# Windowed attention in an encoder block: query preparation and value split placed behind the score products in each step's source order

## The chip, the cores and the metric

The kernel runs on one core of a Trainium2 chip. The metric is the device time of one execution in microseconds (us), as the median of several runs. A core has a TensorE (PE) for matrix products, a VectorE (DVE), a ScalarE (ACT), a GpSimd (POOL) and a queue (SP) from which most DMA transfers are issued. Matrix products write to PSUM, and ACT or DVE must copy the results out before a PSUM tile can be used again.

## What is computed

One block of a bidirectional encoder: 1024 tokens, width 1024, all in float32. The block has a gated linear attention (branch A), a windowed softmax attention (branch B), and a gated feed-forward part. The change lies in branch B:

```python
q = _rope(_rms_norm(q.reshape(bsz, s, SWA_HEADS, hd), q_g), pos)      # 8 heads of 128
k = _rope(_rms_norm(k.reshape(bsz, s, hkv, hd), k_g), pos)            # 2 heads of 128
kc, vc = context(k), context(v)          # blocks of 128 keys: the block before, its own, the next
scores = jnp.einsum("bnqhgd,bnkhd->bnhgqk", qb, kc) * (hd ** -0.5)
scores = jnp.where(mask, scores, -jnp.inf)               # +-128 window
m = jnp.maximum(scores.max(axis=-1, keepdims=True), sink)
p = jnp.exp(scores - m)
denom = p.sum(axis=-1, keepdims=True) + jnp.exp(sink - m)
o = jnp.einsum("bnhgqk,bnkhd->bnqhgd", p / denom, vc)
```

## The kernel before

**Precision.** The products run in a fast float32 form. Each operand is split into a high part (written by ACT) and a low part (the difference, written by DVE), and three products are summed: high by high, high by low, low by high.

**The order of the whole.** The block's input projections come first (partly by a seven-product scheme), then the gated linear attention, then the windowed attention, then the output projections of both branches, then the feed-forward part. Projections that the attention stages need late (queries, keys and values of branch B, a gate of branch A) are kept as generators in a list `dense`; the attention stages draw dense matmuls from it, so that PE has work while a step of the attention waits for other engines.

**The windowed attention (lines 828 to 1040).** It works on 16 units n: two key-value heads g, and eight blocks t of 128 queries, four query heads together. A software pipeline of 22 steps runs them. In step t stand:

- `k_load`, `a_load` (lines 880 and 887): DMA loads of keys, values and queries, for the next steps.
- `k_prep` (892), the split of values: `vSh` on ACT (L894) and `vSl` on DVE (L895), for steps 0 to 7. The parts are read by `a_out` four steps later at the earliest.
- `a_prep` (905), the preparation of the queries of unit t-1: square on ACT (L866), sum over the row on DVE (L867), the inverse root `rs` in two small ACT and four small DVE instructions (L98 to L104), then four DVE operations that apply the norm's gain and the rotation (L912, L914, L916, L917), which write `qn`. The inverse root is not applied to the query; it enters later as the scale of the exponential.
- `a_turn` (919), unit t-2: four transposes of `qn` on PE (L923) into a PSUM tile, then the split `sqh` (ACT, L926) and `sql` (DVE, L927). `k_turn` (897) does the same with the keys of block t-1 (L900, L902, L903).
- `a_scores` (931), unit t-3, four stages, one for each head: three products on PE (L76, the line of the helper `mm`) into a PSUM tile; then one DVE instruction (L941) adds the window's mask, writes the scores `p` to SBUF and takes the row maximum `mx`. The stage of the last head also holds the softmax: small DVE operations on the maxima (L948 to L952), one small and four large exponentials on ACT (L953, L956), the sum `dn` (L958) and its reciprocal `rd` (L960) on DVE, and four multiplications on POOL (L962).
- `a_probs` (964), unit t-5, three stages, one for each key block: four transposes of `p` on PE (L973), then `ph` (ACT, L976) and `pl` (DVE, L977).
- `a_out` (980), unit t-5: six or nine products of probabilities and values (L76), a copy `sob` on ACT (L987), and four DMA stores.

The PSUM tiles of scores, turned queries, turned keys, turned probabilities and outputs come from one pool of four tiles (`ch`); the dense matmuls have four others (`mm`). The scores, the raw queries, the values and `qn` have two buffers each.

**What sets the order.** A list `order` ranks the stages of one step, and `slot` runs them in that rank and puts a share of the step's dense matmuls (15 in steps 2 to 18) behind each stage:

```python
for j, f in enumerate(stages):
    f()
    t = n * (j + 1) // len(stages)
    fill(t - done)
    done = t
```

On PE the instructions stand in just this order (`manual_schedule`). On DVE, ACT, POOL and SP the compiler's planner orders them: it walks through time by its own estimates and gives each engine, whenever it is free, the first instruction in source order whose inputs and buffers are ready. So on these engines the source order is a preference and the result can differ from it; on the chip each engine then runs its list strictly in order. A step has 10 stages in steps 3 and 4, 14 in steps 5 to 7, 12 in step 8, 11 in steps 9 to 15 and 10 in step 16.

Of the kernel before, what the change touches and what calls it, by code (L numbers as in the profile page):

```python
# [30 lines left out]
def body(tc, i, out):  # L31
    nc = tc.nc
    with ExitStack() as root:
# [846 lines left out]
        def k_load(t):  # L880
            raws[t] = sw.tile([P, 256], F32, tag="kvr", name=nm("kvr"))
            need(("skv", t))
            nc.sync.dma_start(out=raws[t], in_=scr["skv", t][:, 256:512])
            keys[t] = sw.tile([P, 2, P], F32, tag="key", name=nm("key"))
            nc.sync.dma_start(out=keys[t].rearrange("p a b -> p (a b)"), in_=scr["key", t])
# [127 lines left out]
        for n in range(2 * KT):  # L1013
# [9 lines left out]
                if n:  # L1023
                    todo[n - 1].append((k_load, n))
            todo[n].append((a_load, g, t))
        order = (a_probs, k_prep, a_prep, a_scores, a_turn, k_turn, a_out, k_load, a_load)
        k_load(0)
        with tc.manual_schedule(engines={mybir.EngineType.PE}):
            for t, v in enumerate(todo):
# [507 lines left out]
```

## Time and profile before

| what | value |
|---|---|
| median of 3 runs | 1645.83 us (1645.22 to 1646.64) |
| profiled execution, its own time | 1645.61 us |
| its span, first to last instruction | 1643.8 us |
| granted TensorE clock, mean | 1.000 |
| DMA, mean over the span | 160 GB/s |
| windowed attention, about | 565 to 740 us |

In the profile a row such as `L76 PE MATMUL ch<-kTh,sqh` names the line, the engine, the operation and the tiles by the program's names without their numbers. The number in square brackets is the idle time of the engine just before the instruction, with the instruction that ended it. In the attention stage step 4 begins on PE at about 581 us, step 5 at 590.7, step 6 at 600.6, step 7 at 611.8, step 8 at 622.7, step 10 at 642.8, step 14 at 678.2 and step 16 at 698.9 (each from step 5 on begins with the transposes L973). Rows of PE overlap, since matmuls are pipelined, so the time that a matmul takes is read from the starts of neighbours.

### The profile page before, as it was taken

Reading aid. Unit: us, or ns where it says so; the run is one execution under the profiler, and the core shown is the slowest. Engines: PE = TensorE matmul, PEld = TensorE weight load, DVE = VectorE, ACT = ScalarE, POOL = GpSimd, SP = SyncE. Lnnn points to the kernel's source line nnn. Section 1 sums busy time; section 2 is a strip of 40 time slices with the busy share of each in tenths; the row PEclk is TensorE's granted clock in tenths of the full one; section 3 lists DMA queues with packets and bytes.
Section 4 is the critical chain, followed back from the end, with each engine's and each line's share of the span. In section 5 each row is a group of like instructions: output and inputs, shape, how many; then the busy total and the mean of one; then the engine's idle time right before and its main releaser. Section 6 shows DMA issues by size and latency. Waiting matters only on the chain.

```text
span 1643.8 us, 23281 instructions
## 1 busy us (share of the span) xinstructions
PE 1626.0 (99%) x7588; PEld 1346.0 (82%) x7588; DVE 1251.4 (76%) x2559; ACT 842.6 (51%) x1762; POOL 76.0 (5%) x68
## 2 busy tenths in 40 slices
PE   9999999999999989999999999999999999999999
PEld 7888888888888778888888888888888888888887
DVE  8866665589986598867885678887777778779655
ACT  8622224468998666665554557333333333354442
POOL 0000000000000034540000000000000000000000
PEclk9999999999999999999999999999999999999999
DMA  7554334475554633248765544443334443596433
GB/s 238 176 178 148 115 122 135 173 250 173 179 161 129 191 108 97 77 138 280 225 205 175 168 146 145 140 149 109 109 115 147 142 147 129 177 341 193 149 98 119
DMA packets 168010, 262.91 MB, mean 160 GB/s; under 512 B 19324, under 2 KB 52860, under 8 KB 167888
## 3 DMA queue, kind: packets, MB, share of 16 engines
q1 hardware_dynamic: 167888, 261.42, 49.8%
q8 instruction: 60, 0.98, 0.2%
q14 instruction: 62, 0.51, 0.1%
HBM read 187.93 MB, written 73.42 MB: 159 GB/s over the span
## 4 chain that ended last, share of the span: by engine, by line
PE 84%; DVE 9%; ACT 4%; DMA 2%; issue 1%; POOL 1%; SPq 0%; ACTq 0%; DVEq 0%
PE mm L76 23%; PE mm L306 9%; PE mm L308 9%; PE mm L307 9%; PE mm L1350 7%; PE ch L1350 5%; PE ch L76 4%; PE ch L306 4%; PE ch L308 4%; PE ch L307 4%; PE ch L460 3%; PE mm L460 2%; ACT p L956 1%; DVE wl L72 1%; DVE cs L655 1%
## 5 line engine op out<-in xcount | busy, mean ns | idle before, releaser
L298 ACT ACTIVATE wh<-ws 128x512 fp32r<-128x512 f32 x132 | 83.3, 632 | 195.9 <-PE mm L307 102.2
L70 ACT ACTIVATE wh<-wr 128x512 fp32r<-128x512 f32 x202 | 124.9, 626 | 87.4 <-PE mm L76 54.9
L72 DVE TENSOR_TENSOR wl<-wr,wh 128x512 fp32r<-128x512 f32 x202 | 137.7, 686 | 26.8 <-ACT wh L70 26.4
L299 DVE TENSOR_TENSOR wl<-ws,wh 128x512 fp32r<-128x512 f32 x132 | 90.5, 686 | 22.7 <-ACT wh L298 22.6
L298 ACT ACTIVATE wh<-wr 128x512 fp32r<-128x512 f32 x69 | 43.6, 632 | 124.8 <-issue 49.7
L962 POOL TENSOR_SCALAR p<-p,rd 128x384 f32<-128x384 f32 (+1 forms) x64 | 75.8, 1202 | 657.1 <-DMA qr<-sq 587.2
L298 ACT ACTIVATE wh<-a 128x512 fp32r<-128x512 f32 x64 | 40.5, 633 | 91.4 <-PE ch L1350 42.3
L76 PE MATMUL mm<-wh,xl 128*128 128x512 f32 x192 | 83.1, 433 | 0.0
L76 PE MATMUL mm<-wh,xh 128*128 128x512 f32 x192 | 79.6, 415 | 0.0
L76 PE MATMUL mm<-wl,xh 128*128 128x512 f32 x192 | 79.6, 414 | 0.0
L299 DVE TENSOR_TENSOR wl<-a,wh 128x512 fp32r<-128x512 f32 x64 | 44.2, 691 | 43.1 <-ACT wh L298 42.5
L1350 PE MATMUL mm<-hh,wh 128*128 128x512 f32 x176 | 68.5, 389 | 0.0
L1350 PE MATMUL mm<-hl,wh 128*128 128x512 f32 x176 | 68.5, 389 | 0.0
L1350 PE MATMUL mm<-hh,wl 128*128 128x512 f32 x176 | 68.5, 389 | 0.0
L76 PE MATMUL mm<-xl,wh 128*128 128x512 f32 x160 | 64.5, 403 | 0.1
L76 PE MATMUL mm<-xh,wh 128*128 128x512 f32 x160 | 64.4, 403 | 0.2 <-ACT wh L70 0.2
L76 PE MATMUL mm<-xh,wl 128*128 128x512 f32 x160 | 59.2, 409 | 0.0
L1320 DVE TENSOR_TENSOR hl<-hr,hh 128x512 fp32r<-128x512 f32 x75 | 51.4, 685 | 3.7 <-ACT hh L1319 3.7
L1350 PE MATMUL ch<-hh,wh 128*128 128x512 f32 x132 | 51.3, 389 | 0.0
L1350 PE MATMUL ch<-hl,wh 128*128 128x512 f32 x132 | 51.3, 389 | 0.0
L1350 PE MATMUL ch<-hh,wl 128*128 128x512 f32 x132 | 51.3, 389 | 0.0
L76 PE MATMUL mm<-oah,wh 128*128 128x512 f32 x128 | 50.2, 392 | 0.0
(620 smaller groups left out, 5077.7 us busy)
## 6 DMA issues: line engine op xcount, KB each, us to landing
wr<-in_w_fi_dram SPq DMA_DIRECT2D x102, 256.0 KB
wr<-in_w_f_dram SPq DMA_DIRECT2D x80, 256.0 KB
wr<-in_w_t_dram SPq DMA_DIRECT2D x56, 256.0 KB
B<-c SPq DMA_DIRECT2D x44, 256.0 KB
T<-tx SPq DMA_DIRECT2D x44, 256.0 KB
a<-in_w_fo_dram SPq DMA_DIRECT2D x44, 256.0 KB
hr<-T SPq DMA_DIRECT2D x44, 256.0 KB
wr<-in_w_ob_dram SPq DMA_DIRECT2D x32, 256.0 KB
```

The costliest lines, as they stand in the source:

```text
L70: nc.scalar.activation(h, raw, AF.Copy)
L72: nc.vector.tensor_tensor(l, raw, h.bitcast(F32), op=ALU.subtract)
L76: nc.tensor.matmul(o, a, b, start=start, stop=stop)
L298: nc.scalar.activation(h, src, AF.Copy)
L299: nc.vector.tensor_tensor(l, src, h.bitcast(F32), op=ALU.subtract)
L306: nc.tensor.matmul(o, h[:, c], x[kk][0], start=start and kk == 0, stop=False, skip_group_check=True)
L307: nc.tensor.matmul(o, h[:, c], x[kk][1], start=False, stop=False, skip_group_check=True)
L308: nc.tensor.matmul(o, l[:, c], x[kk][0], start=False, stop=kk == nk - 1, skip_group_check=True)
L460: nc.tensor.matmul(ys[m], a[:, c], b, start=f0, stop=f1, skip_group_check=True)
L962: nc.gpsimd.tensor_scalar(p[:, h, :w], p[:, h, :w], rd[:, h:h + 1], None, op0=ALU.mult)
L1320: nc.vector.tensor_tensor(l, r, h.bitcast(F32), op=ALU.subtract)
L1350: nc.tensor.matmul(ys[m], a[:, c], b, start=f0, stop=f1, skip_group_check=True)
```

## The change

In each step's source order `k_prep` and `a_prep` stood between the turned probabilities and the scores; now they stand behind the scores.

```diff
-        order = (a_probs, k_prep, a_prep, a_scores, a_turn, k_turn, a_out, k_load, a_load)
+        order = (a_probs, a_scores, k_prep, a_prep, a_turn, k_turn, a_out, k_load, a_load)
```

The functions, their instructions, the buffers, the loop and the number of dense matmuls per step are as before. Because the dense matmuls are shared out by stage, those that stood behind `k_prep` and `a_prep` now stand between the last score product and the turning of the queries.

## Prediction

> **What bounds the kernel now.** I read the page first, then the busy time by stretches, then who waited for whom on the TensorE, then the timelines of the attention stage, engine by engine.
>
> ```profile
> span 1643.8 us, 23281 instructions
> ...
> PE 1626.0 (99%) x7588; PEld 1346.0 (82%) x7588; DVE 1251.4 (76%) x2559; ACT 842.6 (51%) x1762; POOL 76.0 (5%) x68
> ```
>
> PE has work in 99% of the span, so an edit that neither adds PE work nor opens or closes a PE gap is worth nothing. The change touches one stage only, the windowed attention, at about 565 to 740 us. Stretches of it (columns: stretch, length, then busy time and instruction count of PE, PEld, DVE, ACT, POOL, granted clock, DMA share, GB/s):
>
> ```profile
> 580.00:600.00 20.00, 17.18 (x91) 14.15 (x91) 19.17 (x69) 13.36 (x39) 7.48 (x7) 1.00 0.39 113
> 600.00:620.00 20.00, 17.89 (x101) 14.98 (x100) 19.54 (x59) 13.98 (x39) 10.87 (x10) 1.00 0.39 122
> 620.00:640.00 20.00, 19.36 (x107) 16.28 (x106) 18.64 (x65) 13.46 (x37) 10.05 (x9) 1.00 0.28 83
> ```
>
> There are two regimes. From 580 to 620 us DVE is the bound: it is idle for only 0.83 and 0.46 us of two times 20 us, while PE lacks 2.8 and 2.1 us. From 620 us on DVE has 1.4 us in 20 to spare, and PE lacks 0.6. All the waits of PE in the stage are these (waiting line, line waited for, total us, times, longest):
>
> ```profile
> PE ch L76 <- DVE mx L941: 2.6, 5, 0.5
> PE ch L923 <- DVE mx L941: 1.9, 1, 1.9
> PE ch L76 <- DVE pl L977: 1.8, 3, 1.0
> PE ch L973 <- POOL p L962: 0.9, 2, 0.6
> PE ch L76 <- DVE kTl L903: 0.6, 1, 0.6
> PE ch L923 <- DVE qn L917: 0.5, 1, 0.5
> PE ch L923 <- DVE pl L977: 0.5, 1, 0.5
> PE ch L76 <- DVE rd L960: 0.4, 1, 0.4
> ```
>
> They sum to 9.2 us in 15 waits. That is nearly all the stage could give, whatever the order. L76 with "ch" is a score or output product, L923 the turning of the queries, L973 that of the probabilities.
>
> **The change part by part.** *What moves.* Per step of the loop the split of values (k_prep) is one ACT and one DVE instruction; the query preparation (a_prep) is a Square and two small instructions on ACT, and on DVE a reduction, four small operations of the inverse root, two half-width and two full-width operations. Neither holds a matmul or a DMA, so nothing passes the SP queue or POOL's. In step 4 they stand on DVE like this:
>
> ```profile
> 583.10 0.68 DVE L867 TENSOR_REDUCE ss<-sq 128x4 f32<-128x512 f32 x1
> 583.69 0.68 DVE L916 TENSOR_TENSOR qn<-qr,qA 128x512 f32<-128x512 f32 x1
> ...
> 584.70 0.42 DVE L914 TENSOR_TENSOR sq<-qr,qB 128x256 f32<-128x256 f32 x1
> ...
> 587.98 0.55 DVE L941 CUSTOM_DVE_ANT_0 p<-ch,band 128x384 f32<-128x384 f32 x1
> ```
>
> The large DVE operations of one preparation are 3 x 0.68 + 2 x 0.42 = 2.9 us (L917 has the shape of L916, L912 that of L914). The work is the same before and after: 0 us. The count of dense matmuls per step is the same too; only their places among the stages change, since each stage is followed by its share.
>
> *What the order sets.* On PE the source order is the order. A preparation emits no matmul, but its share of dense ones stands behind it, so these move with it from before the four score products to after them: one in steps 9 to 15 (11 stages share 15 matmuls), two in steps 5 to 8 and 16, three in steps 3 and 4 (10 stages), and there these were all that stood ahead of the scores. On the other engines source order is only a preference among what is ready.
>
> *Steps 3 to 7.*
>
> ```profile
> 583.11 0.34 PE L76 MATMUL ch<-kTh,sqh 128*128 128x384 f32 x1
> ...
> 588.60 0.66 PE L923 MATMUL ch<-ident,qn 128*128 128x128 f32 x4 [1.86 <-DVE mx L941]
> ```
>
> In step 4 the first score product is on PE at 583.11, but DVE takes its maximum only at 587.98, with a whole preparation in between; the PSUM tiles of this kind stay full and PE waits 1.86 us. With the maxima ahead of the preparation this wait can go. The second of its kind is the table's 0.5 us of L923 on pl, in step 5. Against that, the scores of step 3 now come three matmuls sooner and wait for the same keys (the table's 0.6 us on kTl). One dense matmul takes 0.23 us, by the starts of neighbours:
>
> ```profile
> 644.86 0.40 PE L76 MATMUL mm<-xl,wh 128*128 128x512 f32 x1
> 645.09 0.40 PE L76 MATMUL mm<-xh,wh 128*128 128x512 f32 x1
> ```
>
> So that wait grows by up to 3 x 0.23 = 0.7 us. Gross: -1.9 - 0.5 + 0.7 = -1.7 us. But DVE has the same work in this stretch, and its idle time from 580 to 620 us is 0.83 + 0.46 = 1.3 us; PE can gain no more unless work is put off past 620 us, and the next step's turning of the queries lets a preparation be late by less than one step. I take -1.3 us; the ends are -2.4 us (both waits gone, nothing added) and +0.7 us (none gone). I stay at the DVE limit because it is the nearest measured one.
>
> *Steps 8 to 16.* Here the preparation is no longer where the source has it:
>
> ```profile
> 642.04 0.68 DVE L867 TENSOR_REDUCE ss<-sq 128x4 f32<-128x512 f32 x1
> ...
> 645.84 0.16 DVE L958 TENSOR_TENSOR dn<-dn,es 128x4 f32<-128x4 f32 x1 [2.25 <-ACT p L956]
> ```
>
> This reduction (the eleventh of sixteen, source place step 11) runs at 642 us, before the scores of step 10: the planner fills DVE's spare time with it, and 2.25 us of idle time still follow. Moving it behind the scores of step 11 in the source can't change its rank against step 10. So I expect the DVE order to stay here, and only the dense matmul to move. That costs, because of a ring: output product, its copy on ACT, four exponentials behind that copy, the sum dn, the first maximum, the second score product.
>
> ```profile
> 642.35 0.59 ACT L987 COPY sob<-ch 128x512 f32<-128x512 f32 x1 [1.96 <-PE ch L76]
> 642.83 0.21 ACT L953 ACTIVATE es<-es 128x4 f32<-128x4 f32 x1
> ...
> 645.02 0.70 ACT L956 ACTIVATE p<-p,nm,rs 128x384 f32<-128x384 f32 x1
> ```
> ```profile
> 645.68 0.40 PE L76 MATMUL mm<-xl,wh 128*128 128x512 f32 x1
> 646.48 0.38 PE L76 MATMUL ch<-kTh,sqh 128*128 128x256 f32 x1 [0.40 <-DVE mx L941]
> ```
>
> The second score product of step 10 starts at 646.48 because the last exponential ends at 645.7 and dn follows. (The gap costs more than the 0.40 shown, since the rows of PE overlap: 0.80 - 0.23 = 0.57 us.) After the change the output product stands one matmul later behind the scores, and its copy with it; the ring is longer by 0.23 us in each step that hangs on it. By the timelines these are steps 10, 11, 15 and 16, so +0.9 us. The ends are 0 and every matmul moved in steps 8 to 16: (7 x 1 + 2 x 2) x 0.23 = 2.5 us. A step that doesn't wait has the same PE work as before and needs no cover.
>
> The sum is -1.3 + 0.9 = -0.4 us. The profiled execution took 1645.61 us (span 1643.8 and 1.8 around it), 0.2 us under the median of 1645.83; on the median the sum is 1645.4 us. The measurement of this kernel can tell about 0.2%, 3.3 us, from no change, so this is none.
>
> *A rule beside a row.*
>
> ```profile
> 682.43 0.44 PE L76 MATMUL ch<-kTh,sqh 128*128 128x384 f32 x1 [0.54 <-DVE mx L941]
> ```
>
> This gap (one of the table's five on mx) is the second score product waiting until the maximum has emptied the first one's PSUM tile; only one dense matmul stands between the two products, before the change and after it. The Trainium skill, page Perfetto Trace Analysis, section Optimization Strategy, says that a gap repeating on the engine that should be saturated can mean that there isn't enough SBUF or PSUM for the next tile. By that rule an order alone gives nothing; the trace agrees for the five gaps on mx, not for the 1.86 us.
>
> **The rivals.**
>
> *Nothing moves.* The gaps are made of PSUM tiles, and DVE's order stays, since the planner ranks only what is ready and places the preparation before the scores are there. For: the five waits on mx are alike (2.6 us in all, longest 0.5), as a fixed latency is. Against: 1.86 us in step 4 is no fixed latency. It gives 0 us, 1645.8.
>
> *Faster.* Where no preparation is about, the exponentials go ahead of the copy:
>
> ```profile
> 708.36 0.71 ACT L956 ACTIVATE p<-p,nm,rs 128x384 f32<-128x384 f32 x1 [1.09 <-DVE es L952]
> ...
> 711.24 0.56 ACT L987 COPY sob<-ch 128x512 f32<-128x512 f32 x1
> ```
> ```profile
> 713.07 0.44 PE L76 MATMUL ch<-kTh,sqh 128*128 128x384 f32 x1 [0.20 <-DVE pl L977]
> ```
>
> The wait after that is 0.20 instead of 0.54 us. If the small operations on the row maxima get ahead of the preparation's 0.68 us ones, eight later steps could look like this: 8 x 0.34 = 2.7, with the -1.3 of the first steps -4.0 us, 1641.8. Against: from step 8 on the preparation is already the lower in rank. The floor is all waits gone, 9.2 + 15 x 0.17 = 11.8 us, 1634.0.
>
> *Slower.* The scores reach PE before what they need, and DVE's order doesn't make up for it. Place: the first product of each step, behind which all dense matmuls of the step queue. Price: every matmul that moves becomes a wait, 2 x 3 in steps 3 and 4, 3 x 2 in 5 to 7, 11 later: 23 x 0.23 = 5.3 us, 1651.1. It decides once DVE's maxima come no sooner than before in steps 3 to 7. For it speaks DVE's 96% and 98% from 580 to 620 us; against it, that a PE gap costs nothing where DVE is the bound.
>
> **How the numbers follow.** The forecast (ends -2.4 and 0.7 + 2.5 = +3.2 us) gets 0.46, nothing moves 0.16, faster 0.21, slower 0.17. The first two lie within 0.2%: 0.62. The likeliest, 1645.4, is the prediction. The range goes from the faster case, 1641.8, rounded down, to past the forecast's upper end of 1649.0: 1641.5 to 1649.5. What lies beyond I put at a third of the faster case and most of the slower one, under 0.2.
>
> **What would show it.** Right: in step 4 the maxima stand ahead of the preparation on DVE and the 1.86 us are smaller; in step 3 the wait on kTl is larger, up to 1.3 us; DVE's idle time from 580 to 620 us is near 0; from 640 us on the preparation stays in its place on DVE, and the second score product waits about 0.2 us longer in steps 10, 11, 15 and 16; the other stages are shifted, not changed. Wrong: exponentials ahead of the copies on ACT from 620 us on (faster), PE waits in the stage of over 12 us (slower), or a PE wait for dense weights, which the stage doesn't have now.

## The result, and the profile after

| what | before | after |
|---|---|---|
| median of 12 runs each, taken in turn | 1645.32 us (1643.94 to 1646.64) | 1641.82 us (1640.88 to 1642.59) |
| ratio after / before | | 0.9978 (95% interval 0.9970 to 0.9986) |
| profiled execution, its own time | 1645.61 us | 1641.89 us |
| its span | 1643.8 us | 1640.1 us |

The change made the kernel 3.5 us faster. This is 0.22%, by the interval between 0.14% and 0.30%. No run of the one kernel reaches the runs of the other, so the difference is clear, though it lies at the border of the 3.3 us that the prediction took as the least that can be told from no change. The forecast was -0.4 us. Its direction is right and the range of the prediction holds the time, but the likeliest case said that no difference would be seen, and 3.1 of the 3.5 us were not in its sum.

The page of the kernel after shows the same work on every engine. PE has the same busy time, in a span that is 3.7 us shorter:

```profile
span 1640.1 us, 23278 instructions
...
PE 1626.0 (99%) x7588; PEld 1346.1 (82%) x7588; DVE 1250.0 (76%) x2559; ACT 841.7 (51%) x1762; POOL 75.5 (5%) x68
```

So PE gaps were closed. The waits of PE between 560 and 760 us, in the kernel after (waiting line, line waited for, total us, times, longest):

```profile
PE ch L76 <- DVE mx L941: 2.1, 4, 0.6
PE ch L76 <- DVE kTl L903: 1.5, 2, 1.0
PE ch L76 <- DVE pl L977: 1.1, 4, 0.4
PE ch L923 <- DVE qn L917: 0.5, 1, 0.5
PE ch L76 <- ACT sob L987: 0.3, 1, 0.3
```

They sum to 5.5 us in 12 waits, where it was 9.2 in 15. The 3.7 us less match the 3.7 us of the span. The large wait of step 4 (L923 on mx, 1.9 us) is gone, and with it the waits for POOL (0.9), for rd (0.4) and of L923 on pl (0.5). The wait for the split keys (kTl) has grown by 0.9 us.

Where in the stage it happened is seen in the stretches of the kernel after (length, then busy time and count of PE, PEld, DVE, ACT, POOL, granted clock, DMA share, GB/s):

```profile
580.00:600.00 20.00, 19.46 (x103) 15.80 (x103) 19.89 (x72) 14.38 (x43) 9.17 (x8) 1.00 0.37 112
600.00:620.00 20.00, 19.38 (x106) 16.10 (x105) 20.00 (x65) 13.12 (x35) 9.92 (x8) 1.00 0.39 114
620.00:640.00 20.00, 19.23 (x106) 16.07 (x105) 19.32 (x66) 14.06 (x41) 10.03 (x8) 1.00 0.31 93
640.00:660.00 20.00, 19.63 (x116) 16.21 (x115) 17.97 (x62) 13.82 (x40) 8.54 (x8) 1.00 0.35 105
```

From 580 to 620 us PE is now busy for 38.84 of 40 us, where it was 35.07. DVE is idle there for 0.11 and 0.00 us. And from 620 to 660 us DVE has more to do than before: 19.32 against 18.64, and 17.97 against 17.18 in this row of the kernel before:

```profile
640.00:660.00 20.00, 19.21 (x110) 16.10 (x110) 17.18 (x60) 13.31 (x36) 7.86 (x8) 1.00 0.30 93
```

DVE is busier in both stretches, so PE did not gain because DVE had less to do there; DVE did other work first. From the start of the turning of step 3 to that of step 7 the kernel before takes 38.73 us, with DVE busy for 37.43, and the kernel after 35.12 us, with DVE busy for 35.01. Of the 3.6 us less, 1.2 are idle time of DVE that was closed and 2.4 are work of DVE that now lies outside these steps.

Which work that was can be counted. L917 is the last operation of a query preparation. The stretches below are cut where PE begins to turn the queries (L923) in steps 4, 7 and 8, and count L917 alone; first the kernel before:

```profile
560.00:588.60 28.60, 2.73 (x4) 1.00 0.62 195
588.60:618.74 30.14, 2.05 (x3) 1.00 0.37 108
618.74:629.17 10.43, 0.67 (x1) 1.00 0.34 105
```

and the kernel after:

```profile
560.00:587.37 27.37, 2.05 (x3) 1.00 0.62 199
587.37:615.88 28.51, 2.04 (x3) 1.00 0.37 104
615.88:626.35 10.47, 1.36 (x2) 1.00 0.38 127
```

Before, four preparations are finished when step 4 turns its queries, one more than are due. After, three are. Three steps later it is still one fewer (six, as many as are due, against seven), and this debt of one preparation is paid between the turnings of steps 7 and 8, where two are finished instead of one. The three steps from one turning to the other took 30.14 us and now take 28.51.

In step 4 the DVE timeline of the kernel after has all four maxima ahead of the preparation (L867 is its first DVE operation):

```profile
583.93 0.56 DVE L941 CUSTOM_DVE_ANT_0 p<-ch,band 128x384 f32<-128x384 f32 x1
...
586.70 0.55 DVE L941 CUSTOM_DVE_ANT_0 p<-ch,band 128x384 f32<-128x384 f32 x1
587.63 0.67 DVE L867 TENSOR_REDUCE ss<-sq 128x4 f32<-128x512 f32 x1
588.22 0.14 DVE L949 TENSOR_TENSOR mx<-mx,sink 128x4 f32<-128x4 f32 x1
588.29 0.68 DVE L916 TENSOR_TENSOR qn<-qr,qA 128x512 f32<-128x512 f32 x1
```

The start of the turning, compared step by step, gives a running account (from one profiled execution of each kernel): the difference after minus before is +0.37 us in step 2, +0.75 in step 3, -1.23 in step 4, -1.40, -1.90 and -2.86 in steps 5 to 7, and from there nearly level, -2.67 in step 9 and -3.22 in step 17. So steps 3 to 7 gave 2.86 + 0.37 = 3.2 us, steps 8 to 17 another 0.4. The output projections then start 3.54 us sooner.

### The profile page after: what moved, and what is told of

It is laid out like the page before. It is cut to its first block, busy times and chain, and to the rows that moved or that the text cites. A ratio compares the mean times of both kernels' runs of the same rounds, so it can differ in the third digit from the quotient of the medians.

```text
span 1640.1 us, 23278 instructions
## 1 busy us (share of the span) xinstructions
PE 1626.0 (99%) x7588; PEld 1346.1 (82%) x7588; DVE 1250.0 (76%) x2559; ACT 841.7 (51%) x1762; POOL 75.5 (5%) x68
## 4 chain that ended last, share of the span: by engine, by line
PE 84%; DVE 10%; ACT 3%; DMA 1%; issue 1%; SPq 0%; ACTq 0%; DVEq 0%
PE mm L76 23%; PE mm L306 9%; PE mm L308 9%; PE mm L307 9%; PE mm L1350 7%; PE ch L1350 5%; PE ch L76 4%; PE ch L308 4%; PE ch L307 4%; PE ch L306 4%; PE ch L460 3%; PE mm L460 2%; ACT p L956 1%; DVE wl L72 1%; DVE cs L655 1%
## 5 line engine op out<-in xcount | busy, mean ns | idle before, releaser
L962 POOL TENSOR_SCALAR p<-p,rd 128x384 f32<-128x384 f32 (+1 forms) x64 | 75.3, 1195 | 654.4 <-ACT wh L70 585.6
```

What stands on the lines that cost most here:

```text
L962: nc.gpsimd.tensor_scalar(p[:, h, :w], p[:, h, :w], rd[:, h:h + 1], None, op0=ALU.mult)
```

## The experiments

The theory after the result: the gain comes from the order on DVE, where what PE waits for now stands ahead of a preparation that isn't due. The rival: it comes from PE's own order, in which dense matmuls now stand behind the scores, or from a lighter DVE. Each difference below is that of the medians, against the kernel before on the same chip; a running account is that of the turnings, as above. The source order ranks the work of ACT as it does that of DVE, and no run moves it on one of the two alone. Where the text speaks of DVE's order, it goes by the rows and waits.

**The two halves of the change.** The change moves two things, the source order (for DVE, ACT and POOL) and the places of dense matmuls (on PE). Each was made alone. `e1` keeps the source order of before and gives PE the order of after:

```diff
+        moved = (a_probs, a_scores, k_prep, a_prep, ...)
+                ranked = sorted(v, key=lambda e: moved.index(e[0])) or [None]
+                share = {e: n * (j + 1) // len(ranked) - n * j // len(ranked) for j, e in enumerate(ranked)}
...
+                    if scored and e[0] in (k_prep, a_prep):
+                        held += share[e]          # filled behind the last a_scores
```

> Only the dense matmuls move: PE's order is that of the changed kernel, the source order of the stages that of the kernel before. Theory 1 (the gain of 3.5 us is DVE's order: in steps 3 to 7 the row maxima get ahead of the query preparation): no gain, between 0 and +1.5 us, with the 1.9 us wait of the turning in step 4 still there or grown. Theory 2 (the gain comes from the dense matmuls that now stand behind the scores): -2.5 to -3.5 us.

Measured: 1646.15 us, +0.6 us, ratio 1.0005 (0.9996 to 1.0014). The matmuls' places give no gain. On DVE, step 4 of e1 still has the preparation ahead of the maxima:

```profile
583.74 0.68 DVE L867 TENSOR_REDUCE ss<-sq 128x4 f32<-128x512 f32 x1
584.33 0.68 DVE L916 TENSOR_TENSOR qn<-qr,qA 128x512 f32<-128x512 f32 x1
585.67 0.55 DVE L941 CUSTOM_DVE_ANT_0 p<-ch,band 128x384 f32<-128x384 f32 x1
```

But the expectation that the 1.9 us wait would stay or grow was wrong. With the moved matmuls to run, PE turns the queries of step 4 without a wait, 1.17 us ahead of the kernel before, nearly as in the change (1.23). Two steps later it is 1.13 us behind. The last maximum of step 4 starts on DVE at 590.11, where it was 589.41 before and 586.70 in the change, and PE now waits at other places, longest here:

```profile
602.77 0.33 PE L973 MATMUL ch<-ident,p 128*128 128x128 f32 x1 [1.11 <-POOL p L962]
```

So to fill the one large wait is not the gain. The time is lost again one and two steps later.

`e2` is the other half: the new source order, with each dense matmul at its old place.

```diff
-        order = (a_probs, k_prep, a_prep, a_scores, ...)
+        order = (a_probs, a_scores, k_prep, a_prep, ...)
...
+                    if scored and e is scored[0]:
+                        fill(sum(share[x] for x in v if x[0] in (k_prep, a_prep)))   # shares by the old order
```

> Only the source order moves: PE's order is that of the kernel before, instruction by instruction. Theory 1 (DVE's order): -2.5 to -4.5 us, all of the gain or more, since the scores of step 3 don't come early any more and the wait for the keys stays at 0.6 us. Theory 2 (places of the dense matmuls): -1 us or less.

Measured: 1641.73 us, -3.9 us, ratio 0.9977 (0.9969 to 0.9986). This half has the whole gain. The waits of PE in e2 sum to 5.3 us, near the 5.5 of the change, but they are others:

```profile
PE ch L76 <- DVE pl L977: 2.4, 5, 0.7
PE ch L76 <- DVE mx L941: 1.6, 3, 0.5
PE ch L973 <- POOL p L962: 0.7, 2, 0.5
PE ch L923 <- DVE qn L917: 0.6, 1, 0.6
```

There is no wait for kTl, not even the 0.6 us of the kernel before, which the expectation had left standing. The waits for pl are longer (2.4 us against 1.1). The two halves add up to -3.3 us, the change to -3.5.

**The early and the late steps.** `e3` uses the new order in steps below 8 alone, `e4` in steps from 8 on alone:

```diff
-                v.sort(key=lambda e: order.index(e[0]))
+                v.sort(key=lambda e: (moved if t < 8 else order).index(e[0]))     # e4: t >= 8
```

> The new order in steps 0 to 7 alone. Theory 1 (DVE bound from 580 to 620 us, so the gain is made in steps 3 to 7): -2.7 to -3.5 us. Theory 3 (the gain needs the later steps, where the exponentials now go ahead of the copies): -1.5 us or less. By the prediction's bound (only DVE's idle time of 1.3 us can be won): -1.3 us.

> The new order from step 8 on alone. The prediction's ring (output, copy, exponentials, sum, maximum): +0.9 us. Theory 1: between -0.5 and +1 us, no change that can be measured. Theory 3 (exponentials ahead of the copies): -1.5 to -3 us.

Measured: e3 1643.42 us, -2.2 us, ratio 0.9987 (0.9978 to 0.9996); e4 1645.74 us, +0.2 us, ratio 1.0005 (0.9996 to 1.0014). The late steps alone give nothing, so the gain is made in the early ones. But e3 falls between its expectations and is short of the change by 1.3 us. Its turning is 1.55 us ahead of before in step 7 and 0.50 in step 9, so 1.05 us were given back in steps 8 and 9. There the old source order puts the preparation ahead of the scores again, while one is still owed. On DVE its reduction (L867, 0.68 us at 624.17) stands ahead of the split of the probabilities (L977, at 624.85). The stretch of e3, and PE's largest wait in it:

```profile
620.00:640.00 20.00, 18.36 (x102) 15.41 (x101) 19.47 (x62) 13.68 (x38) 9.90 (x8) 1.00 0.30 92
```
```profile
625.56 0.44 PE L76 MATMUL ch<-kTh,sqh 128*128 128x384 f32 x1 [1.07 <-DVE pl L977]
```

PE is busy for 18.36 us here, against 19.23 in the change and 19.36 before. The reading is that the debt has to be paid in an order that lets PE's work pass.

The running account bears this out. From the turning of step 7 to that of step 17 e3 loses 1.09 us with the old order, and the change gains 0.36 with the new one; both owe a preparation. In e4 none is owed, and there the new order loses 0.63. So in these runs the new order helps in the late steps only where work has been put off. e4 also has the exponentials ahead of the copies in steps 9 to 11 (Theory 3), and no gain from it.

**Which of the two stages.** `e5` moves only the split of values behind the scores, `e6` only the preparation of queries:

```diff
+        order = (a_probs, a_prep, a_scores, k_prep, a_turn, ...)      # e5
+        order = (a_probs, k_prep, a_scores, a_prep, a_turn, ...)      # e6
```

> Only the split of values moves behind the scores. Per step it is 0.42 us on DVE, the query preparation 2.9 us and more. Theory 1 (the row maxima gain by the DVE time that stands behind them now): 0 to -0.8 us. Rival (any of the two will do, since what counts is that the scores come earlier): -2 us or more.

> Only the query preparation moves behind the scores. Theory 1: nearly the whole gain, -2.7 to -3.8 us. Rival as for the values alone: about as much as these give.

Measured: e6 1642.27 us, -3.4 us, ratio 0.9979 (0.9971 to 0.9988); e5 1643.97 us, -1.7 us, ratio 0.9990 (0.9982 to 0.9999). The queries alone give what the change gives. The values alone, one DVE operation of 0.42 us in a step, gave more than was expected of them. Its preparations are finished as early as before (four by step 4), and the turning of queries in step 4 no longer waits for mx; the turning of keys behind it (L900, at 588.84) waits for mx instead, for 1.10 us where it was 1.86. The two do not add up (-5.1 against -3.5), as if they removed the same wait, in part or whole. Each of these two edits also moves the dense matmuls behind its stage, so they don't part DVE's order from PE's; in e1 the matmuls' places alone took the wait of step 4 away for a time.

**Further behind.** `e7` puts both stages behind the output products in every step, `e10` only the preparation of queries and only in steps below 8:

```diff
+        order = (a_probs, a_scores, a_turn, k_turn, a_out, k_prep, a_prep, k_load, a_load)            # e7
+        first = (a_probs, a_scores, k_prep, a_turn, k_turn, a_out, a_prep, k_load, a_load)            # e10, t < 8
```

> Both go further back, behind turning and output. If the gain is work put off past 620 us into steps where DVE has time to spare, a still later rank gives as much or more: -3.5 to -5 us. Rival (the preparation then comes too late for the turning in the next step, and PE waits for qn): -2 to +1 us.

> The change, and in steps 0 to 7 the query preparation behind the output products too. If what is won is preparation put off, and the run with both stages behind the output in all steps lost by its later steps and a load at the entry: -4 to -5 us. Rival (one preparation put off is all that the turning in the next step allows): as the change, -3 to -3.7 us, or less where the preparations pile up in step 8.

Measured: e7 1643.74 us, -1.9 us, ratio 0.9988 (0.9979 to 0.9997); e10 1641.49 us, -3.9 us, ratio 0.9975 (0.9965 to 0.9985). The median of e10 is the lowest of all, but it can't be told from the change. In e10 the turning of step 7 is 3.47 us ahead of before (2.86 in the change), and in step 9 it is 2.62 ahead. In e7 it is 3.32 ahead in step 7 and 1.75 in step 9. So whatever more is put off is given back when it falls due, and e7 gives back 1.6 us.

That is not all that e7 loses. Ahead of the turning of step 2 PE waits for a load (the profile names that of the values), which it doesn't in the change:

```profile
567.03 0.41 PE L900 MATMUL ch<-ident,key 128*128 128x128 f32 x2 [2.13 <-DMA kvr<-skv]
```

That turning is 1.01 us behind the kernel before, in the change 0.37. From there to step 7 e7 gains 4.33 us, more than the change's 3.23. The number of e7's rival came out, but not its reason: PE waits for qn for 0.2 us in all.

**A lighter DVE.** `e8` is the change with the low part of the values computed on POOL; `e11` does the same in the kernel before:

```diff
-            nc.vector.tensor_tensor(vSl[t], v2, vSh[t].bitcast(F32), op=ALU.subtract)
+            nc.gpsimd.tensor_tensor(vSl[t], v2, vSh[t].bitcast(F32), op=ALU.subtract)
```

> The change, and the low part of the values computed on POOL instead of DVE, which takes 8 x 0.42 = 3.3 us off DVE in steps 0 to 7. If DVE is still the bound there after the change (idle for 0.1 us in 40), PE wins a further 1 to 2 us: -4.5 to -5.5 us against the kernel before. Rival (what is left of PE's waits is the latency of PSUM tiles, and DVE's load doesn't matter): as the change, -3.5 us.

> The kernel before with its own order, and only the low part of the values on POOL: 3.3 us less for DVE in steps 0 to 7, PE's order untouched. If DVE's load is the bound there (the prediction's bound): -1.5 to -3 us. If the order is what counts, since the planner fills the time set free with preparations that aren't due: 0, within 1 us.

Measured: e8 1644.19 us, -1.5 us, ratio 0.9991 (0.9982 to 0.9999); e11 1647.64 us, +2.3 us, ratio 1.0010 (1.0001 to 1.0019). Taking 8 x 0.416 = 3.3 us of work off DVE (L895) helped neither kernel. By the medians e8 is 2.0 us slower than the change and e11 2.3 slower than the kernel before, but most of the 2.3 goes with the clock. Seven of e11's eleven runs had a granted clock of 0.998 or 0.999; its four runs at 1.000 have a median of 1646.04 us, and the 21 of the kernel before at 1.000 one of 1645.28. At the same clock e11 is 0.8 us slower, which is within the 1 us of its second expectation. Neither expectation for e8 held. In e8, DVE is as full as in the change:

```profile
580.00:600.00 20.00, 18.60 (x100) 15.27 (x99) 19.88 (x67) 13.74 (x40) 10.68 (x10) 1.00 0.32 99
600.00:620.00 20.00, 19.07 (x104) 16.04 (x103) 19.82 (x68) 13.29 (x37) 9.93 (x8) 1.00 0.38 114
```

The planner filled what came free with preparations that weren't due: by the turning of step 7 seven are finished, as in the kernel before, and not six. Up to there e8 gains as much as the change (3.20 us from the turning of step 2, against 3.23). From there to the turning of step 17 it loses 0.59, about as e4 does with nothing owed, where the change gains 0.36. In e11 DVE is less full than before, and PE is idle for more (2.2 and 3.1 us, where it was 2.8 and 2.1):

```profile
580.00:600.00 20.00, 17.81 (x93) 14.04 (x92) 18.88 (x71) 13.66 (x37) 7.35 (x8) 1.00 0.37 109
600.00:620.00 20.00, 16.93 (x92) 13.74 (x91) 18.11 (x55) 13.68 (x37) 11.24 (x10) 1.00 0.34 100
```

From the turning of step 2 to that of step 5 e11 gains 1.3 us on the kernel before, and in the next step it loses 2.0. What grew there are the waits of PE for the multiplications on POOL (L962), from 0.9 to 2.4 us in the stage. POOL itself is free: the last split is done by 583 us and the first multiplication starts at 588.34. It's the reciprocal on DVE (L960) that comes late: in step 5 it starts at 597.80, where it was 596.08 in the kernel before, although PE turns the queries of this step only 0.11 us later. The sum dn, which it needs, waits for the exponentials, and the last of these ends 1.4 us later. Ahead of them on e11's DVE the reduction of a preparation (L867) stands before the last operation on the row maxima (L952):

```profile
591.73 0.67 DVE L867 TENSOR_REDUCE ss<-sq 128x4 f32<-128x512 f32 x1
...
592.39 0.15 DVE L952 TENSOR_TENSOR es<-sink,mx 128x4 f32<-128x4 f32 x1
```

In the kernel before it stood behind:

```profile
591.41 0.16 DVE L952 TENSOR_TENSOR es<-sink,mx 128x4 f32<-128x4 f32 x1
591.48 0.68 DVE L867 TENSOR_REDUCE ss<-sq 128x4 f32<-128x512 f32 x1
```

On ACT two splits of probabilities (L976) stand ahead of these exponentials, where it was one. So with 1.1 and 1.9 us of idle DVE in these stretches, what holds PE up is not a lack of DVE time. The order on DVE and ACT is the reason that these rows suggest; that is argued from them and not shown by a run of its own. That DVE is slower beside a split on POOL isn't excluded as a part: in e11 one small operation (L101, at 578.92) took 0.71 us there, where the median is 0.16, while the large ones kept their time (L867 took 0.67 us beside a split in e8).

**A wider step between two score products.** `e9` is the change with one dense matmul more between the first and the second score product in the steps where one stood there, taken from behind the preparation where it can be, for the gaps on mx that repeat in the late steps:

```diff
+                if at and share[at[0]] == 1:
...
+                    share[at[0]] += 1
+                    share[give[0]] -= 1
```

> The change, and in each step one dense matmul more between the first and the second score product, taken from behind the preparation. If the gaps of 0.5 to 0.6 us there are the fixed time from the first score product to its maximum (the page's rule on repeating gaps), each shrinks by 0.23 us: about 7 of them, -1.6 us more than the change, -5.1 us. Rival (the ring over output copy and exponentials sets the second score product, so the matmul only fills the front of the same wait): 0 to -0.5 us more than the change, about -3.7 us.

Measured: 1643.46 us, -1.9 us, ratio 0.9991 (0.9982 to 1.0000). Both expectations were missed. Where the edit adds a matmul, the gaps shrank as a gap of fixed end does: in steps 14 and 15 from 0.60 and 0.58 us to 0.32 and 0.36. In steps 8 and 16 two matmuls stood there already, and the gaps stay (0.57 and 0.35). Here is that of step 14, and a loss at the other end of the stage:

```profile
678.82 0.44 PE L76 MATMUL ch<-kTh,sqh 128*128 128x384 f32 x1 [0.32 <-DVE mx L941]
...
729.88 0.50 PE L76 MATMUL ch<-pl,vSh 128*128 128x512 f32 x1 [0.94 <-DVE pl L977]
```

All waits of PE sum to 6.7 us, against 5.5 in the change. The new ones are one of 0.94 us at 729.88, where an output product waits for the low probabilities, 0.83 for pl at 602.66, and 1.2 us in all for POOL. Up to the turning of step 17 e9 is still 0.4 us ahead of the change in these profiles (3.60 us ahead of before, against 3.22), so its loss lies behind that. Why a matmul moved within a step brings these is not settled.

## Why the prediction was wrong, and where it was right

**The step that failed** is the cap in steps 3 to 7: "DVE has the same work in this stretch, and its idle time from 580 to 620 us is 0.83 + 0.46 = 1.3 us; PE can gain no more unless work is put off past 620 us". The exception in this sentence is what happened. I read 96% and 98% of busy time as a bound, and took -1.3 us. Steps 3 to 7 gave -3.2. One preparation, 2.9 us of large DVE operations, stood in this stretch without being due, and the new order puts it off until step 8, where DVE had 1.4 us in 20 to spare. That makes a cap of about 1.3 + 2.9 = 4.2 us, and 3.2 lie within it; from the turning of step 3 to that of step 7, 1.2 us came from idle time and 2.4 from work put off. I had the rows for it: the rank of preparations was known to run ahead (the prediction shows that of step 11 before the scores of step 10), and a count of L917 up to the turning of step 4 would have shown four where three were due.

The Trainium skill, page Perfetto Trace Analysis, section Optimization Strategy, says that where a kernel has regimes with different most-contended engines, interleaving these regimes may improve it. I had named the two regimes and then treated them as closed. The count of L917 above agrees with the rule: work went from the regime in which DVE is full into the one in which it isn't.

**Gross terms of these steps.** The two waits that I let go (1.9 on mx, 0.5 on pl) did go. That alone is no proof of the working: the 1.9 went in e1 too, and nothing was gained there. The wait for kTl in step 3 was to grow by up to 0.7 us. It grew from 0.6 to 1.04, and a second of 0.42 us came in step 5:

```profile
577.28 0.38 PE L76 MATMUL ch<-kTl,sqh 128*128 128x256 f32 x1 [1.04 <-DVE kTl L903]
...
591.88 0.44 PE L76 MATMUL ch<-kTl,sqh 128*128 128x384 f32 x1 [0.42 <-DVE kTl L903]
```

So the gross sum, -1.7, was itself too small, since waits of other kinds (0.9 for POOL, some of those for pl) went as well. With DVE's order set by what PE needs, it isn't one wait that goes.

**Steps 8 to 16.** I forecast +0.9 us by the ring, and the account gives -0.4. The term exists. Where no preparation is owed it comes out near its size: from the turning of step 7 to that of step 11 both e1 and e4 lose 0.96 us (and get 0.3 back by step 17). In the change these steps cost nothing. The list of steps was not right either: step 14, whose gap the prediction shows, hangs on the ring too, and the waits that were to grow by 0.2 us in steps 10, 11, 15 and 16 went from 0.40, 0.39, 0.54 and 0.60 us to 0.36, none, 0.58 and 0.35. Between the second score product of step 14 and the copy of the same step's output lay 688.21 - 682.43 = 5.78 us, and now 685.20 - 679.19 = 6.01, which is the 0.23 us of one dense matmul. The copy on ACT in the kernel after, and behind it DVE's end of the ring:

```profile
685.20 0.59 ACT L987 COPY sob<-ch 128x512 f32<-128x512 f32 x1 [1.96 <-PE ch L76]
```
```profile
688.69 0.16 DVE L958 TENSOR_TENSOR dn<-dn,es 128x4 f32<-128x4 f32 x1 [2.25 <-ACT p L956]
688.81 0.56 DVE L941 CUSTOM_DVE_ANT_0 p<-ch,band 128x384 f32<-128x384 f32 x1
689.29 0.08 DVE L941 DVE_READ_ACCUMULATOR2_ANT mx<- 128x1 f32 x1
689.29 0.17 DVE L960 RECIPROCAL rd<-dn 128x4 f32<-128x4 f32 x1
```

In the kernel before, the reciprocal stood ahead of the maximum:

```profile
691.70 0.16 DVE L958 TENSOR_TENSOR dn<-dn,es 128x4 f32<-128x4 f32 x1 [2.25 <-ACT p L956]
691.89 0.18 DVE L960 RECIPROCAL rd<-dn 128x4 f32<-128x4 f32 x1
692.02 0.56 DVE L941 CUSTOM_DVE_ANT_0 p<-ch,band 128x384 f32<-128x384 f32 x1
```

From dn to the maximum it took 0.32 us and now takes 0.12. The turn of the ring, from one second score product to the next, is 692.64 - 682.43 = 10.21 us before and 689.43 - 679.19 = 10.24 after. My working had the right price for the matmul and no place for a reordering among the small operations.

**The rival that names the time.** "Faster" gave 1641.8 us, and 1641.82 was measured, but its sum was made of other parts (-1.3 early, -2.7 late). Its mechanism, which the prediction gave as a sign of being wrong, is there in part. In step 9 the exponentials are ahead of the copy, where the copy was first before:

```profile
639.10 0.71 ACT L956 ACTIVATE p<-p,nm,rs 128x384 f32<-128x384 f32 x1 [1.37 <-DVE es L952]
...
641.98 0.56 ACT L987 COPY sob<-ch 128x512 f32<-128x512 f32 x1
```

They are so in steps 5, 6 and 8 to 11 (in step 8 before as well) and not in 12 to 15, and the turnings of the late ones show no such gain: -2.86 us in step 7, -2.87 in step 11. In e4 the same order in steps 9 to 11 gained nothing. A forecast's number that comes out isn't yet its reason.

**What was right.** DVE's idle time from 580 to 620 us is near 0 (0.11 us). The wait of step 4 is gone with the maxima ahead. The dense matmuls' move alone gains nothing (e1, +0.6 us, which is not clear of zero; the rival "slower" had priced it at 5.3). No PE wait for dense weights came. The rule of the Trainium skill on repeating gaps (page Perfetto Trace Analysis, section Optimization Strategy), which the prediction cites, fits the four gaps on mx that the change left (2.1 us). No run here gave these tiles another buffer, so whether that would close them wasn't tried.

**What stays open.** How far the gain is DVE's order and how far ACT's. Why the values alone (e5) shorten the large wait while four preparations are still done early; the matmuls' places are one candidate. And what makes e9 slower than the change, and e8 by more than the 1.2 us of its profiled execution. The variants also reach the turning of step 2 at different times in their profiles, e4 0.44 and e3 1.38 us behind before, though neither edit changes the source order ahead of it (the profiled execution of e3 took 1644.77 us, the longest of its runs). From there on the accounts are steadier: e4, whose edit begins with step 8, stays between 0.16 and 0.25 us behind in steps 3 to 8. So a difference of about 1 us between the totals of two variants isn't explained by its edit alone.

## What to carry to other kernels

A full engine is a bound only for work that is due: before you cap a gain by its idle time, count how much of what it does in that stretch is needed only later, and whether a later stretch has room for it. On engines that run their lists in order, put what the bottleneck engine waits for ahead of what can wait, and keep that order until the debt is paid. A change that moves the source order also moves the fill work, so test the two apart.

## What the runs showed of the hardware

The split of one block of values (128x256) takes 0.416 us on DVE (median in the kernel before). On POOL, in e8, its median is 0.908 us and its longest 1.234 (min, median and max in ns, then the first and last start):

```profile
L895 POOL TENSOR_TENSOR vSl<-kvr,vSh x8: 737/908/1234, 566.2 to 580.5; 128x256 fp32r<-128x256 f32 x8
```

POOL is idle at that time, so the slower operation delays nothing on its own engine, and still the move didn't pay.
